# Where operands lie: split weights shifted by 0 to 28 bytes from unit to unit, rows of moving operands a multiple of 256 bytes apart

## The chip, the cores and the metric

The kernel runs on one core of a Trainium2 chip. The metric is the device time of one execution in microseconds (us); less is better. A NeuronCore has a matrix engine (PE, with its weight loads shown as PEld), VectorE (DVE), ScalarE (ACT), GpSimd (POOL) and SyncE (SP). SP and POOL issue nearly all the DMAs here. SBUF is the on-chip memory, 128 partitions wide; an address below is a byte offset within each partition.

## The reference

Two layers of a decoder trunk on 528 tokens (16 learned meta tokens, then 512) with 1024 channels, in float32. Each layer is a half-step SwiGLU feed-forward block, a mixer, and a second half-step SwiGLU block; layer 0 mixes by retention, layer 1 by gated linear attention (GLA):

```python
for i in range(DEPTH):                      # 2
    h = h + 0.5 * swiglu(rmsnorm(h, norm_ffn1[i]), ffn1_w_in[i], ffn1_w_out[i])
    hn = rmsnorm(h, norm_mix[i])
    mix = retention(hn, ...) if i % 2 == 0 else gla(hn, ...)
    h = h + mix
    h = h + 0.5 * swiglu(rmsnorm(h, norm_ffn2[i]), ffn2_w_in[i], ffn2_w_out[i])
h = rmsnorm(h, final_norm)[:, N_META:]

def swiglu(x, w_in, w_out):
    gate, up = jnp.split(x @ w_in, 2, axis=-1)      # 2 x 2816 columns
    return (jax.nn.silu(gate) * up) @ w_out
```

Nearly all the arithmetic is in products of the 528 token columns with weight matrices.

## The kernel before

**Products.** Each fp32 operand is split into a high part in the type fp32r and a low part that is the remainder, also in fp32r. A product of two 128-row blocks is then three matmuls, recorded by the helper `mm3`: high weights by high data (L402), high weights by low data (L403), low weights by high data (L404). Most have 264 moving columns, half of the 528 tokens; in the last feed-forward block they have 256, in GLA 256 or 272. Each matmul has a weight load of 128 columns of its own, so the order on PE is load, matmul, load, matmul, the next load running while a matmul streams.

**Units.** A two-by-two block product (two weight blocks, two halves of the tokens) is done with seven products instead of eight, by the Strassen-Winograd sums. The seven are named `a11, s1, s2, a12, s3, s4, a22`. Their weights are sums of weight blocks, made by GpSimd DMAs that add while they copy and by DVE (L166, L168). Their moving operands are, for three of them, plain rows of the normalized stream (`uha` and `ula`, 8 rows of 528 columns), and for four of them sums over blocks of it, `n3, t1, t2, t4`, kept in `th` (high) and `tl` (low) as `[P, 4, 4, 264]`, the first 4 the row `k` of the product, the second 4 which of the sums. On the way out of a feed-forward block the hidden activations are kept likewise, seven sums of 264 columns in a tile `H` (`hf` in the profile) with the high parts in front and the low parts behind. One product of a unit with four rows `k` is 12 matmuls in the order k = 0 high, low, high; k = 1 high, low, high; and so on.

**Weights.** The class `Weights` streams them. `plan` lists the products' weights in the order of use. `_load` issues a 256 KB DMA on SP into one of `raw_bufs=7` tiles `raw` (and into three `pair` tiles for the sums) as soon as a tile is free. `_split` turns each into a high tile `whi` by an ACT cast (L160) and a low tile `wlo` by a DVE subtraction (L161), four products ahead of PE. There are seven tiles of each, 512 columns of 4 bytes each.

**Addresses.** A row of 264 columns is 1056 bytes, that is 4 x 256 + 32. A row of 528 columns is 2112 bytes, 8 x 256 + 64. The rows `k` of `th` and `tl` are 4224 bytes apart, 16 x 256 + 128, and the low half of `H` lies 7392 bytes behind the high half, 28 x 256 + 224. A weight tile is 2048 bytes and a weight block of 128 columns 512 bytes. In the program as built, all weight blocks of the products start at a multiple of 64 bytes (nearly all of them at a multiple of 256), and all their moving rows at a multiple of 32. What follows calls the difference between the start of a matmul's moving row and the start of the weights that are loaded while it streams, modulo 256 bytes, the relative place of that matmul.

**Order.** The program is recorded in the order of the code with a scheduler that moves urgent instructions ahead; each engine then runs its own instructions in order and waits on semaphores. `causal`, a triangular mask, and `ctail`, three small pieces of it, are loaded and copied once at the start (L355 to L359) and used by retention alone. `half_neg`, eight columns of -0.5, is the exponent for the reciprocal root that POOL computes in the norms.

Of the kernel before, what the change touches and what calls it, by code (L numbers as in the profile page):

```python
# [10 lines left out]
F32 = mybir.dt.float32  # L11
# [3 lines left out]
ALU = mybir.AluOpType  # L15
# [36 lines left out]
BY_P = ((16, 128, 4, 512), (0, 128, 1, 16))  # L52
PW = 512
AHEAD = 4
HEAD_START = 300
# [7 lines left out]
class Weights:  # L63
# [72 lines left out]
    def _split(self, upto):  # L136
        V = self.nc.vector
        while self.split < min(upto, len(self.plan)):
# [80 lines left out]
def trunk(ctx, tc, a):  # L219
# [5 lines left out]
    upool = ctx.enter_context(tc.tile_pool(name="upool", bufs=1))  # L225
    tmp = ctx.enter_context(tc.tile_pool(name="tmp", bufs=2))
    acc = ctx.enter_context(tc.tile_pool(name="acc", bufs=2, space=bass.MemoryType.PSUM))
    W = Weights(tc, ctx)


# [123 lines left out]
    nc.sync.dma_start(ident, a["tri"][0])  # L354
    causal = const.tile([P, P], F32, name="causal")  # L355
    nc.sync.dma_start(causal, a["tri"][1])
    ctail = const.tile([3 * MR, MR], F32, name="ctail")
    for g in range(3):
        S.copy(ctail[g * MR:(g + 1) * MR], causal[g * MR:(g + 1) * MR, g * MR:(g + 1) * MR])  # L359
    ones_r = const.tile([P, P], F32R, name="ones")  # L360
# [13 lines left out]
    uh, ul = [[t[:, d, :] for d in range(KD)] for t in (uha, ula)]  # L374
    rb = upool.tile([P, T], F32, tag="rb", name="rb")
    rc = upool.tile([P, 8], F32, tag="rc", name="rc")

# [60 lines left out]
    def rsqrt_rows(sq, parts, width, name, finish):  # L438
# [10 lines left out]
        ms = tmp.tile([P, 8], F32, tag="ms", name=f"ms_{name}")  # L449
        V.tensor_scalar(ms[:w, :nj], st[:w, :nj], 1.0 / width, EPS, ALU.mult, ALU.add)  # L450
        r = tmp.tile([P, 8], F32, tag="r", name=f"r_{name}")
        G.tensor_tensor(r[:w, :nj], ms[:w, :nj], half_neg[:w, :nj], ALU.pow)
        dg = tmp.tile([P, T], F32, tag="hf", name=f"dg_{name}")
# [11 lines left out]
    def enter(gcol, by, lag=1, lag2=1):  # L465
# [52 lines left out]
        def stats():  # L518
# [12 lines left out]
            for (b0, w, nb, m), c in zip(by, cols):  # L531
                ms = tmp.tile([P, 8], F32, tag="ms", name=f"ms_{name}{c}")
                V.tensor_scalar(ms[:w, :nb], st[:w, c:c + nb], 1.0 / D, EPS, ALU.mult, ALU.add)
                r = rc[:w, c:c + nb]
                G.tensor_tensor(r, ms[:w, :nb], half_neg[:w, :nb], ALU.pow)
# [106 lines left out]
    def quarters(halves, th, tl):  # L642

        tl = tl if isinstance(tl, list) else [tl[:, k] for k in range(4)]
        wd = width(halves)

        def rhs(what, k):
# [3 lines left out]
            i = ("n3", "t1", "t2", "t4").index(what)  # L651
            return th[:, k, i, :wd], tl[k][:, i, :wd]

# [3 lines left out]
    def ffn(which, layer, halves, gcol, feed, late=False):  # L657
# [4 lines left out]
        wd = a1 - a0  # L662
        with tc.tile_pool(name=f"h_{me}", bufs=4) as hp, tc.tile_pool(name=f"t_{me}", bufs=1) as tp, \
# [24 lines left out]
            def sums(j):  # L688
                norm(j)
                for i in range(2):  # L690
                    k = 2 * j + i
                    u_sums(up_, f"{me}{k}", halves, normed[j][:, i].rearrange("p h t -> p (h t)"), th[:, k], tl[:, k])

# [16 lines left out]
            def hidden(f, y, part=None):  # L710
# [265 lines left out]
    def out_last(key, hh, hl, halves, scale):  # L976
# [77 lines left out]
        with tc.issue_after(ins.ins):  # L1054
            for d in range(KD - 4, KD):
                turn(d)
        ms = tmp.tile([P, 8], F32, tag="ms", name="ms_fb")
        V.tensor_scalar(ms[:, :2], st[:, :2], 1.0 / D, EPS, ALU.mult, ALU.add)
        r = tmp.tile([P, 8], F32, tag="r", name="r_fb")
        G.tensor_tensor(r[:, :2], ms[:, :2], half_neg[:, :2], ALU.pow)  # L1060
        for b in range(2):
# [14 lines left out]
    def retention(feed):  # L1076
        with tc.tile_pool(name="retp", bufs=1) as rp, tc.tile_pool(name="wmore", bufs=2) as wp, psum_pool(4) as pp:
# [14 lines left out]
            def sums(k):  # L1092
# [7 lines left out]
                u_sums(rp, f"r{k}", HALVES, un.rearrange("p h t -> p (h t)"), th[:, k], tl[:, k])  # L1100

# [16 lines left out]
            def head(h):  # L1118
# [289 lines left out]
    def gla(feed):  # L1408
        with tc.tile_pool(name="glap", bufs=1) as gp, psum_pool(2) as pp, \
# [4 lines left out]
            for k in range(4):  # L1414
                nc.sync.dma_start(spilt[k], xs[k])
            th = gp.tile([P, 4, 4, 264], F32R, tag="th", name="gth")
            tl, normed = [], []
# [4 lines left out]
            def sums(k):  # L1422
# [15 lines left out]
                tl.append(resid.tile([P, 4, 264], F32R, tag=f"x{k}", name=f"gtl{k}"))  # L1438
                split(th[:, k, :2], tl[k][:, :2], t01)
                split(th[:, k, 2:], tl[k][:, 2:], t23)  # L1440

# [640 lines left out]
```

## Time and profile before

| | |
|---|---|
| median of 3 runs | 2070.59 us (2070.3 to 2073.34) |
| profiled execution, its own time | 2071.41 us |
| its span on the core | 2069.6 us |
| granted TensorE clock | 0.999 of full |
| PE busy | 2057.5 us (99%), 16335 matmuls |
| PEld busy | 2012.9 us (97%), 16335 loads |
| DVE busy | 1790.8 us (87%) |
| ACT busy | 1200.2 us (58%) |
| DMA | 318.84 MB, mean 154 GB/s |

The profile is of one execution. A matmul's recorded duration (about 285 ns) is its passage through the array and overlaps with its neighbours', so the rate at which PE works is not read from durations or from busy time, but from the distance between starts of successive matmuls. The chain of waits is followed back from the last instruction; a chain that is nearly all PE means that a microsecond saved elsewhere is worth nothing unless PE waits for it.

### The profile page before, as it was taken

To read this page: it belongs to the slowest core of one execution; us is meant where nothing else is said; L and a number is where in the kernel's file an instruction comes from. 1 tells how busy PE (TensorE), PEld (TensorE's weight loads), DVE (VectorE), ACT (ScalarE), POOL (GpSimd) and SP (SyncE) were. 2 spreads that over 40 slices of the span, in tenths; PEclk is the share of its full clock that TensorE was granted. 3 is DMA by queue.
4 is the path that set the end of the run, shared out by engine and by line. 5 is a ranking of instruction groups with operands and counts; after the bars stand their busy time and mean duration, and the time that the engine had idled before them with its cause. 6 is when DMAs were issued, how large, how long until landed. Compare 5 with 4: busy or idle time off the path is not lost.

```text
span 2069.6 us, 42946 instructions
## 1 busy us (share of the span) xinstructions
PE 2057.5 (99%) x16335; PEld 2012.9 (97%) x16335; DVE 1790.8 (87%) x3218; ACT 1200.2 (58%) x2365; POOL 208.8 (10%) x181
## 2 busy tenths in 40 slices
PE   9999999999999999999999999999999999999998
PEld 9999999999999999999999999999999988999998
DVE  8988889978686889988889998889897968998886
ACT  5756566554545455656666565666645445666664
POOL 1011111010101000111111011111001000111110
PEclk9999999999999999999999999999999999999999
DMA  7676777355555532776776476677614351687772
GB/s 224 154 193 158 193 185 185 107 144 132 146 132 138 136 104 70 184 191 158 195 188 172 111 180 179 162 197 177 194 57 119 91 165 61 161 214 174 183 179 72
DMA packets 176112, 318.84 MB, mean 154 GB/s; under 512 B 17569, under 2 KB 40737, under 8 KB 175905
## 3 DMA queue, kind: packets, MB, share of 16 engines
q1 hardware_dynamic: 133856, 237.04, 34.6%
q0 software_dynamic: 40896, 75.51, 23.5%
q10 hardware_dynamic: 1152, 3.55, 0.5%
q8 instruction: 128, 2.10, 0.4%
q14 instruction: 80, 0.65, 0.1%
HBM read 311.76 MB, written 4.26 MB: 153 GB/s over the span
## 4 chain that ended last, share of the span: by engine, by line
PE 95%; DVE 2%; ACT 1%; issue 1%; DMA 0%; POOL 0%; SPq 0%; POOLq 0%; ACTq 0%; DVEq 0%
PE po_r L403 2%; PE po_r L402 2%; PE po_r L404 2%; PE Xf20o L402 1%; PE Xf10o L402 1%; PE Xf11o L402 1%; PE Xf10o L404 1%; PE Xf10o L403 1%; PE Xf20o L403 1%; PE Xf20o L404 1%; PE Xf11o L403 1%; PE Xf11o L404 1%; PE lv L1614 1%; PE Xf20u L402 1%; PE Xf11u L402 1%; PE Xf21u L404 1%
## 5 line engine op out<-in xcount | busy, mean ns | idle before, releaser
L160 ACT CAST whi<-raw 128x512 fp32r<-128x512 f32 (+1 forms) x893 | 525.6, 606 | 482.3 <-DVE raw L166 92.2
L161 DVE TENSOR_TENSOR wlo<-raw,whi 128x512 fp32r<-128x512 f32 (+1 forms) x893 | 584.1, 669 | 143.8 <-ACT whi L160 134.7
L160 ACT CAST whi<-pair 128x512 fp32r<-128x512 f32 (+1 forms) x304 | 183.5, 604 | 122.2 <-PE Xf11u L403 7.3
L161 DVE TENSOR_TENSOR wlo<-pair,whi 128x512 fp32r<-128x512 f32 (+1 forms) x304 | 202.0, 664 | 6.4 <-ACT whi L160 5.0
L129 POOL DMA_DIRECT2D pair<-in_f_in x73 | 88.5, 1213 | 725.4 <-DVE wlo L161 313.6
L166 DVE TENSOR_TENSOR raw<-pair,raw 128x512 f32<-128x512 f32 (+1 forms) x146 | 97.3, 667 | 2.6
L168 DVE TENSOR_TENSOR raw<-raw,raw 128x512 f32<-128x512 f32 (+1 forms) x146 | 97.3, 666 | 2.5
L129 POOL DMA_DIRECT2D pair<-in_f_out x44 | 53.2, 1208 | 379.1 <-DVE wlo L161 208.8
L402 PE MATMUL po_r<-ogh,whi 128*128 128x264 f32 x256 | 73.0, 285 | 0.0
L403 PE MATMUL po_r<-ogl,whi 128*128 128x264 f32 x256 | 73.0, 285 | 0.0
L404 PE MATMUL po_r<-ogh,wlo 128*128 128x264 f32 x256 | 72.8, 285 | 0.0
L129 POOL DMA_DIRECT2D pair<-in_ret_in x20 | 24.3, 1215 | 301.8 <-DVE wlo L161 90.7
L402 PE MATMUL Xf20o<-hf,whi 128*128 128x264 f32 x176 | 50.8, 289 | 0.2
L402 PE MATMUL Xf11o<-hf,whi 128*128 128x264 f32 x176 | 50.8, 289 | 0.2
L402 PE MATMUL Xf10o<-hf,whi 128*128 128x264 f32 x176 | 50.8, 289 | 0.2
L403 PE MATMUL Xf10o<-hf,whi 128*128 128x264 f32 x176 | 50.0, 284 | 0.0
L403 PE MATMUL Xf11o<-hf,whi 128*128 128x264 f32 x176 | 50.0, 284 | 0.0
L403 PE MATMUL Xf20o<-hf,whi 128*128 128x264 f32 x176 | 50.0, 284 | 0.0
L404 PE MATMUL Xf10o<-hf,wlo 128*128 128x264 f32 x176 | 49.9, 284 | 0.0
L404 PE MATMUL Xf11o<-hf,wlo 128*128 128x264 f32 x176 | 49.9, 284 | 0.0
L404 PE MATMUL Xf20o<-hf,wlo 128*128 128x264 f32 x176 | 49.9, 284 | 0.0
L402 PEld LDWEIGHTS po_r<-ogh,whi 128*128 128x128 f32 x256 | 48.3, 189 | 0.0
(1007 smaller groups left out, 8523.8 us busy)
## 6 DMA issues: line engine op xcount, KB each, us to landing
raw<-in_f_in SPq DMA_DIRECT2D x277, 256.0 KB, 4.5
pair<-in_f_in SPq DMA_DIRECT2D x150, 256.0 KB, 4.7
pair<-in_f_in POOLq DMA_DIRECT2D x73, 512.0 KB, 6.7
raw<-in_f_out SPq DMA_DIRECT2D x80, 256.0 KB, 3.7
raw<-in_ret_in SPq DMA_DIRECT2D x76, 256.0 KB, 3.3
raw<-in_f_out SPq DMA_DIRECT2D x72, 192.0 KB, 3.2
pair<-in_f_out SPq DMA_DIRECT2D x48, 256.0 KB, 3.9
pair<-in_f_out POOLq DMA_DIRECT2D x24, 512.0 KB, 6.1
```

What stands on the lines that cost most here:

```text
L129: nc.gpsimd.dma_start(t, aps[2].unsqueeze(1).broadcast_to([P, 2, n]), accum_op=ALU.add)
L160: self.nc.scalar.copy(hi[:, :n], raw)
L161: V.tensor_sub(lo[:, :n], raw, hi[:, :n].bitcast(F32))
L166: V.tensor_add(s2, self.tiles[c][:, 1], self.tiles[c, "a11"])
L168: V.tensor_add(raw, raw, s2)
L402: nc.tensor.matmul(ps, lhsT=lh, rhs=rh, start=start, stop=False, **kw)
L403: nc.tensor.matmul(ps, lhsT=lh, rhs=rl, start=False, stop=False, **kw)
L404: return nc.tensor.matmul(ps, lhsT=ll, rhs=rh, start=False, stop=stop, **kw)
L1614: nc.tensor.matmul(ps[:, j, J * P:J * P + n], lhsT=Kt[:, j, J * P:(J + 1) * P], rhs=q, start=(J == 0), stop=(J == 3), skip_group_check=True)
```

## The change

The tiles of the split weights get 8 columns more, 2080 bytes (8 x 256 + 32), and the part that is used starts `c % 8` columns of 4 bytes inside, where `c` counts the units; so all seven products of a unit are shifted by the same 0 to 28 bytes and the next unit by 4 more. Plain (non-unit) weights are not shifted. A tile `wskew` of 32 bytes between the high and the low tiles gives both the same place modulo 256. `th` and `tl` become four tiles each, of 1088 columns (4352 bytes, 17 x 256), so that the rows `k` of one sum lie a multiple of 256 bytes apart; `H` gets 1856 columns a half (7424 bytes, 29 x 256), so that its low part has the place of its high part. The four rows of the head outputs `og` get 16 columns more each. Fillers of 96 and 224 bytes stand behind `th` and `tl`, in the feed-forward blocks and in retention. What this costs in memory is taken from `raw_bufs` (7 to 6), from `causal` and `ctail`, which now live in retention's own pool and are loaded when it is entered, and from `half_neg`, whose exponent is now one column of `rc`. Pools are opened in another order. Number and sizes of matmuls, casts and subtractions are unchanged.

```diff
+SKEW = 4 * 264 + 32
+HW = 7 * 264 + 8
+RSKEW = 56
...
-    def __init__(self, tc, ctx, raw_bufs=7, pair_bufs=3, bufs=7):
+    def __init__(self, tc, ctx, raw_bufs=6, pair_bufs=3, bufs=7):
...
-            hi = home[0].tile([P, PW], F32R, tag="hi", name=f"whi{i}")
-            lo = home[0].tile([P, PW], F32R, tag="lo", name=f"wlo{i}")
+            o = c % 8 if order else 0
+            hi = home[0].tile([P, PW + 8], F32R, tag="hi", name=f"whi{i}")[:, o:o + PW]
+            if i == 0:
+                self.pool.tile([P, 8], F32, tag="skew", name="wskew", bufs=1)
+            lo = home[0].tile([P, PW + 8], F32R, tag="lo", name=f"wlo{i}")[:, o:o + PW]
...
-    half_neg = const.tile([P, 8], F32, name="half_neg")
-    V.memset(half_neg, -0.5)
+    V.memset(rc[:, 7:8], -0.5)
+
+    def rsqrt(r, ms):
+        G.tensor_tensor(r, ms, rc[:r.shape[0], 7:8].broadcast_to(list(r.shape)), ALU.pow)
+
+    def slices(pool, tag, name):
+
+        return [pool.tile([P, SKEW], F32R, tag=f"{tag}{k}", name=f"{name}{k}")[:, :4 * 264]
+                .rearrange("p (i t) -> p i t", i=4) for k in range(4)]
...
-            th, tl = [tp.tile([P, 4, 4, 264], F32R, tag=f"t{i}", name=f"t{i}{me}") for i in "hl"]
+            th, tl = [slices(tp, f"t{i}", f"t{i}{me}") for i in "hl"]
+            tp.tile([P, 24], F32, tag="skew", name=f"skew{me}")
...
-                    h = hp.tile([P, 2, 7, 264], F32R, tag="H", name=f"h{me}{f}")
+                    h = hp.tile([P, 2, HW], F32R, tag="H", name=f"h{me}{f}")[:, :, :7 * 264]
+                    h = h.rearrange("p i (q t) -> p i q t", q=7)
...
-            th, tl = [rp.tile([P, 4, 4, 264], F32R, tag=f"t{i}", name=f"rt{i}") for i in "hl"]
+            th, tl = [slices(rp, f"t{i}", f"rt{i}") for i in "hl"]
+            causal = rp.tile([P, P], F32, tag="causal", name="causal")
+            nc.sync.dma_start(causal, a["tri"][1])
+            ctail = rp.tile([3 * MR, MR], F32, tag="ctail", name="ctail")
+            for g in range(3):
+                S.copy(ctail[g * MR:(g + 1) * MR], causal[g * MR:(g + 1) * MR, g * MR:(g + 1) * MR])
+            rp.tile([P, RSKEW], F32, tag="skew", name="rskew")
...
-                    og[h] = [rp.tile([P, 4, T], F32R, tag="v" + i, name=f"og{i}{h}") for i in "hl"]
+                    og[h] = [rp.tile([P, 4, T + 16], F32R, tag="v" + i, name=f"og{i}{h}")[:, :, :T] for i in "hl"]
```

In the program as built, the three-matmul products keep their order on PE but for two swaps of a few matmuls (in the first feed-forward block and in retention's first head). In both kernels 14,872 of the fp32r matmuls have 256 to 272 columns. By relative place in eighths of 256 bytes (from 0 to 31, 32 to 63 and so on) they number 1719, 2072, 1679, 2033, 1723, 2010, 1625, 2011 before, each eighth then holding one place only, its lower end; and 2136, 1751, 2548, 1569, 2003, 1722, 1765, 1378 in the changed kernel, where any multiple of 4 bytes occurs.

On SP, at the entry to GLA, before (the numbers behind `raw` count the raw loads in order of use; `spill` saves the residual stream):

```order
L132 DMA raw422_19534<-in_f1_out 128x512
L123 DMA pair172_19913<-in_gla_in 128x512 x2
L132 DMA raw423_19575<-in_f1_out 128x512
L132 DMA raw424_19594<-in_gla_in 128x512
L123 DMA pair173_20147<-in_gla_in 128x512 x2
L132 DMA raw425_19670<-in_gla_in 128x512
L132 DMA raw426_19714<-in_gla_in 128x512
L132 DMA raw427_19733<-in_gla_in 128x512
L1415 DMA spill0_19987<-x0_79 128x1056
L1415 DMA spill1_19988<-x1_80 128x1056
```

and in the changed kernel:

```order
L135 DMA raw421_19566<-in_f1_out 128x512
L126 DMA pair172_19945<-in_gla_in 128x512 x2
L135 DMA raw422_19607<-in_f1_out 128x512
L135 DMA raw423_19626<-in_f1_out 128x512
L126 DMA pair173_20182<-in_gla_in 128x512 x2
L135 DMA raw424_19702<-in_gla_in 128x512
L135 DMA raw425_19746<-in_gla_in 128x512
L135 DMA raw426_19765<-in_gla_in 128x512
L1432 DMA spill0_20019<-x0_85 128x1056
L1432 DMA spill1_20020<-x1_86 128x1056
```

Every raw load is issued one place later against the rest of the queue, since it needs a tile that one release more has to free.

On ACT, at the entry to retention, before (`rb` is the row of reciprocal roots that the norm needs):

```order
L489 ACTIVATE sq_n2_7_4941<-x3_82 128x528
L160 CAST whi232_5001<-raw112_4844 128x512
L160 CAST whi233_5007<-raw113_4863 128x512
L160 CAST whi234_5013<-raw114_4881 128x512
L160 CAST whi235_5062<-raw115_4905 128x512
L160 CAST whi236_5108<-raw116_4929 128x512
L546 COPY rb_137<-bc_n2_0_5068 128x512
```

and in the changed kernel:

```order
L499 ACTIVATE sq_n2_7_4946<-x3_88 128x528
L166 CAST whi232_5019<-raw112_4868 128x512
L166 CAST whi233_5025<-raw113_4886 128x512
L1098 COPY ctail_4973<-causal_4971 32x32 x3
L166 CAST whi234_5031<-raw114_4910 128x512
L166 CAST whi235_5080<-raw115_4934 128x512
L556 COPY rb_133<-bc_n2_0_5086 128x512
```

The three small copies of the mask, which stood among the first casts of the program, now stand between two weight casts, and wait for the mask's DMA, which SP issues just ahead of retention's tables `ropeq` and `ropek`; one weight cast that stood ahead of `rb` now stands behind it.

More of the change, by code (lines that the diff above doesn't have):

```diff
@@ L225, in trunk @@
     upool = ctx.enter_context(tc.tile_pool(name="upool", bufs=1))
-    tmp = ctx.enter_context(tc.tile_pool(name="tmp", bufs=2))
+    small = ctx.enter_context(tc.tile_pool(name="small", bufs=2))
     acc = ctx.enter_context(tc.tile_pool(name="acc", bufs=2, space=bass.MemoryType.PSUM))
     W = Weights(tc, ctx)
+    rows = ctx.enter_context(tc.tile_pool(name="rows", bufs=1))
+    tmp = ctx.enter_context(tc.tile_pool(name="tmp", bufs=2))
     def ffn_steps(last, late):
@@ L354, in trunk @@
     nc.sync.dma_start(ident, a["tri"][0])
[L355 to L359, printed above, removed]
     ones_r = const.tile([P, P], F32R, name="ones")
@@ L374, in trunk @@
     uh, ul = [[t[:, d, :] for d in range(KD)] for t in (uha, ula)]
-    rb = upool.tile([P, T], F32, tag="rb", name="rb")
-    rc = upool.tile([P, 8], F32, tag="rc", name="rc")
+    rb = rows.tile([P, T], F32, tag="rb", name="rb")
+    rc = rows.tile([P, 8], F32, tag="rc", name="rc")
+    V.memset(rc[:, 7:8], -0.5)
[4 more added lines that the diff above has]
+                .rearrange("p (i t) -> p i t", i=4) for k in range(4)]
     def urgent():
@@ L448, in rsqrt_rows @@
                              start=(j == 0), stop=(j == nj - 1), skip_group_check=True)
-        ms = tmp.tile([P, 8], F32, tag="ms", name=f"ms_{name}")
+        ms = small.tile([P, 8], F32, tag="ms", name=f"ms_{name}")
         V.tensor_scalar(ms[:w, :nj], st[:w, :nj], 1.0 / width, EPS, ALU.mult, ALU.add)
         r = tmp.tile([P, 8], F32, tag="r", name=f"r_{name}")
-        G.tensor_tensor(r[:w, :nj], ms[:w, :nj], half_neg[:w, :nj], ALU.pow)
+        rsqrt(r[:w, :nj], ms[:w, :nj])
         dg = tmp.tile([P, T], F32, tag="hf", name=f"dg_{name}")
@@ L531, in stats @@
             for (b0, w, nb, m), c in zip(by, cols):
-                ms = tmp.tile([P, 8], F32, tag="ms", name=f"ms_{name}{c}")
+                ms = small.tile([P, 8], F32, tag="ms", name=f"ms_{name}{c}")
                 V.tensor_scalar(ms[:w, :nb], st[:w, c:c + nb], 1.0 / D, EPS, ALU.mult, ALU.add)
                 r = rc[:w, c:c + nb]
-                G.tensor_tensor(r, ms[:w, :nb], half_neg[:w, :nb], ALU.pow)
+                rsqrt(r, ms[:w, :nb])
                 n = m // nb
@@ L642, in quarters @@
     def quarters(halves, th, tl):
-        tl = tl if isinstance(tl, list) else [tl[:, k] for k in range(4)]
         wd = width(halves)
@@ L662, in ffn @@
         wd = a1 - a0
[L663 removed]
+        with tc.tile_pool(name=f"t_{me}", bufs=1) as tp, tc.tile_pool(name=f"h_{me}", bufs=4) as hp, \
                 tc.tile_pool(name=f"u_{me}", bufs=3) as up_, psum_pool(4) as pp:
             other["pool"] = pp
[L666 removed]
+            th, tl = [slices(tp, f"t{i}", f"t{i}{me}") for i in "hl"]
+            tp.tile([P, 24], F32, tag="skew", name=f"skew{me}")
             rhs_in = quarters(halves, th, tl)
@@ L1056, in out_last @@
                 turn(d)
-        ms = tmp.tile([P, 8], F32, tag="ms", name="ms_fb")
+        ms = small.tile([P, 8], F32, tag="ms", name="ms_fb")
         V.tensor_scalar(ms[:, :2], st[:, :2], 1.0 / D, EPS, ALU.mult, ALU.add)
         r = tmp.tile([P, 8], F32, tag="r", name="r_fb")
-        G.tensor_tensor(r[:, :2], ms[:, :2], half_neg[:, :2], ALU.pow)
+        rsqrt(r[:, :2], ms[:, :2])
         for b in range(2):
@@ L1415, in gla @@
                 nc.sync.dma_start(spilt[k], xs[k])
-            th = gp.tile([P, 4, 4, 264], F32R, tag="th", name="gth")
+            th = slices(gp, "th", "gth")
             tl, normed = [], []
```

10 lines of the change are left out of this document (5 added, 5 removed).

## Prediction

> **What bounds the kernel now.** I read the page first, for the shares and the chain, then windows without a stall, for the rate of PE, then the timeline of single products, for what that rate depends on, and last the waits and DMA issues at the two places where the change moves an instruction.
>
> From the page: busy time of PE, its weight loads and DVE, the chain, and the two costliest groups.
>
> ```profile
> PE 2057.5 (99%) x16335; PEld 2012.9 (97%) x16335; DVE 1790.8 (87%) x3218; ACT 1200.2 (58%) x2365; POOL 208.8 (10%) x181
> ...
> PE 95%; DVE 2%; ACT 1%; issue 1%; DMA 0%; POOL 0%; SPq 0%; POOLq 0%; ACTq 0%; DVEq 0%
> ...
> L160 ACT CAST whi<-raw 128x512 fp32r<-128x512 f32 (+1 forms) x893 | 525.6, 606 | 482.3 <-DVE raw L166 92.2
> L161 DVE TENSOR_TENSOR wlo<-raw,whi 128x512 fp32r<-128x512 f32 (+1 forms) x893 | 584.1, 669 | 143.8 <-ACT whi L160 134.7
> ```
>
> The chain is PE for 95% of the span: only the rate of PE and the few places where PE waits count. The rate stands in windows inside layers 0 and 1 in which every matmul has 264 columns (busy time and count of PE, PEld, DVE, ACT, POOL, then the granted clock):
>
> ```profile
> 900.00:980.00 80.00, 80.00 (x659) 80.00 (x659) 69.14 (x118) 47.84 (x92) 9.69 (x8) 1.00 0.69 169
> 1235.00:1315.00 80.00, 80.00 (x660) 80.00 (x659) 67.48 (x113) 46.30 (x89) 9.66 (x8) 1.00 0.70 177
> ```
>
> 80 us over 659 matmuls, of which one or two only reach in at an edge, is 121.5 ns from start to start, at the full clock and without a gap. Times 14,872 matmuls of 256 to 272 columns this is 1807 us, 87% of the span. One ns in that distance is 14.9 us, or 0.7%; the 0.2% that a measurement of this kernel can tell from no change is 4.1 us, or 0.28 ns.
>
> Is the distance a constant? The weight load alone doesn't set it: in a run of ten products with 128 moving columns (from the chain: start, us, count) a load and a matmul take 109 ns together, less than 121.5.
>
> ```profile
> 512.78 1.09 PE tv L1237 x10
> ```
>
> So the moving stream sets it, and where operands lie shows in it. The timeline of PE (start, recorded duration) for the product of `t4` in two units of the same block: the same 12 matmuls on the same rows of `th`, at relative places 96, 224, 96, 224 for k = 0 to 3. First matmul of the product and first one after it; of the second unit the first six too. Last, a product of `t2` (places 64 and 192) and of `t1` (32 and 160).
>
> ```profile
> 1172.19 0.28 PE L402 MATMUL Xf11u<-thf,whi 128*128 128x264 f32 x1
> ...
> 1173.64 0.28 PE L402 MATMUL Xf11g<-uha,whi 128*128 128x264 f32 x1
> ...
> 1192.63 0.29 PE L402 MATMUL Xf11u<-thf,whi 128*128 128x264 f32 x1
> 1192.75 0.29 PE L403 MATMUL Xf11u<-tlf,whi 128*128 128x264 f32 x1
> 1192.88 0.29 PE L404 MATMUL Xf11u<-thf,wlo 128*128 128x264 f32 x1
> 1193.01 0.28 PE L402 MATMUL Xf11u<-thf,whi 128*128 128x264 f32 x1
> 1193.13 0.28 PE L403 MATMUL Xf11u<-tlf,whi 128*128 128x264 f32 x1
> 1193.25 0.28 PE L404 MATMUL Xf11u<-thf,wlo 128*128 128x264 f32 x1
> 1193.37 0.29 PE L402 MATMUL Xf11u<-thf,whi 128*128 128x264 f32 x1
> ...
> 1194.11 0.28 PE L402 MATMUL Xf11g<-uha,whi 128*128 128x264 f32 x1
> ...
> 1176.57 0.28 PE L402 MATMUL Xf11g<-thf,whi 128*128 128x264 f32 x1
> ...
> 1178.03 0.28 PE L402 MATMUL QZf11g<-uha,whi 128*128 128x264 f32 x1
> ...
> 1185.33 0.29 PE L402 MATMUL QZf11u<-thf,whi 128*128 128x264 f32 x1
> ...
> 1186.80 0.28 PE L402 MATMUL Xf11u<-thf,whi 128*128 128x264 f32 x1
> ```
>
> The twelve take 1.45, 1.48, 1.46 and 1.47 us: 120.8, 123.3, 121.7 and 122.5 ns each. Within the slow one the three at place 96 take 0.38 us (127 ns each) and the next three, at 224, 0.36 us (120 ns). So there is something to win or lose here, the place has to do with it, and the same places can run in a fast or in a slow pattern. It is also little: the fastest of these products lies 0.7 ns under the mean, the slowest 1.8 ns over it.
>
> A rule of the Trainium skill speaks to this. "TensorE: Matmul & The Clock Gate", in "Step-by-step: what each phase is for", gives PE two independent SBUF read ports, one for the moving operand and one for weight loads, so that a load doesn't slow the running matmul; by that rule the place of one against the other can't matter, and this change does nothing to the rate. The same page's "Back-to-back issue gap" would put a matmul of 264 columns at 264/2.4 + 2.5 = 112.5 ns. The trace disagrees with both here: 121.5 ns, and 120 against 127 by place.
>
> **The change part by part.**
>
> *The places of the operands.* No matmul, load, cast or subtraction is added or taken away; what can change is the 121.5 ns. In the old program the relative place is always one of the eight multiples of 32 and goes through all of them about evenly (1625 to 2072 matmuls each); the four products above visit six of the eight. In the new one it goes through all multiples of 4, again about evenly (1378 to 2548 in an eighth), because the shift goes round by units and the weight tiles themselves now step by 32 bytes. If the distance depends on the place smoothly, the mean over an even round is the same sum with finer steps: change 0. What the trace can't show is a place that isn't a multiple of 32, since the old program has none. I bound it by the products above: all 14,872 at the rate of the fastest, (120.8 - 121.5) x 14,872 = -10 us; all at the rate of the slowest, (123.3 - 121.5) x 14,872 = +27 us. I take 0: the change picks no place, it spreads them.
>
> *Shifted weights on ACT and DVE.* 1197 casts and as many subtractions now write to addresses that aren't multiples of 32. I take their 606 and 669 ns as unchanged. If they grew by 5%, DVE would gain 40 us of work, spread over 279 us in which it is idle, and PE waits for weights hardly anywhere: cost 0, as long as DVE stays under 100%.
>
> *One raw tile fewer.* SP waits with raw loads for a free tile nearly all the time, up to 23.8 us for one, and a load lands 4.5 us after its issue (SP queue's waits, in all, times, longest; DMA issues):
>
> ```profile
> SPq L132 <- DVE raw L168: 882.3, 140, 23.8
> ...
> raw<-in_f_in SPq DMA_DIRECT2D x277, 256.0 KB, 4.5
> ```
>
> A unit takes 84 x 121.5 ns = 10.2 us and uses three raw tiles, so a tile is worth 3.4 us of lead, and seven are 24 us. A tile is held from its landing through the four products of splitting ahead, some 6 us, and an `a12` until `s4` is made, some 4 us more; with six tiles 20 - 10 - 4.5 leaves about 6 us to spare inside a block. Cost 0 there. At the entry to GLA the cover is thin already. ACT's casts in a row, its wait for a raw load, and the chain there (start, us):
>
> ```profile
> 1466.67 2.71 ACT L160 CAST whi<-raw 128x512 fp32r<-128x512 f32 x5
> ...
> 1472.36 0.62 ACT L160 CAST whi<-raw 128x512 fp32r<-128x512 f32 x1 [2.27 <-DMA raw<-in_gla_in]
> ...
> 1468.01 4.27 DMA raw<-in_gla_in
> ```
>
> ```profile
> 1465.00:1470.00 5.00, 5.00 (x43) 5.00 (x43) 5.00 (x10) 4.30 (x10) 0.00 (x0) 1.00 0.79 246
> 1470.00:1475.00 5.00, 5.00 (x37) 4.69 (x37) 4.01 (x8) 2.73 (x7) 1.20 (x1) 1.00 0.90 293
> 1475.00:1480.00 5.00, 4.06 (x27) 3.49 (x26) 3.25 (x8) 2.54 (x5) 1.71 (x2) 1.00 1.06 360
> ```
>
> This DMA is the one on the chain; behind it PE starts 37 and 27 matmuls in 5 us instead of 43. With six tiles the load waits for one release more. Casts follow each other every 0.54 us there, so +0.5 us is what I take; the ends are 0, if another load is the late one, and 1.5, if the release waits for a whole product.
>
> *The mask at retention's entry.* SP issues one small DMA more ahead of the tables, and the queue behind it (the tables, then six raw loads) moves by an issue of 0.33 us. ACT's three copies wait for its landing; behind them stand two weight casts and `rb`. In the old run, the tables' issue on SP, ACT's cast that would be next, and PE in these windows:
>
> ```profile
> 355.99 0.33 SPq L1090 DMA_DIRECT2D ropeq<-in_rope  x1
> ...
> 358.19 1.64 ACT L160 CAST whi<-raw 128x512 fp32r<-128x512 f32 x3
> 361.89 0.62 ACT L160 CAST whi<-raw 128x512 fp32r<-128x512 f32 x1 [2.06 <-PE pq L403]
> ```
>
> ACT stands 2.06 us here for PE to free a tile, so the copies (0.6 us) and a landing up to 361.9, that is 5.9 us after issue, are hidden: 0. End: +1.5, if the mask lands later. The three copies and the DMA that go from the start of the program were beside PE's start-up work: 0.
>
> Sum against the profiled execution's own 2071.41: 0 + 0.5 = 2071.9. That execution lies 0.8 above the median of the runs, 2070.59, so I forecast 2071 for the median.
>
> **The rivals.**
>
> *A slow place that lasts (slower).* In the old layout a product leaves its place after every third matmul: 96, 224, 96, 224 above. With rows 256 bytes apart and the low parts on the places of the high ones, all 12 matmuls of a product keep one place, so a product that comes to lie near 96 stays at 127 ns, and one near 224 at 120. The rows moved so (`th`, `tl`, `H`) carry some 8600 matmuls. If a quarter of these run at 126 instead of 121.5 ns and a quarter at 120: 2150 x 4.5 - 2150 x 1.5 = +6.5 us, 2077; if slow patterns also catch their neighbours, half of them at 126, +16 us, 2087. For it: the 0.38 us above, and that the slow pattern returns at k = 2 in that same product. Against it: with the same rows the first unit ran in 1.45 us. It decides from a mean of +0.28 ns on.
>
> *Off the 32-byte steps it runs smoother (faster).* All old places are multiples of 32, and a slow pattern may need them: two streams that go through the memory in step. If the shift breaks it, products run like the fastest, 120.8 ns: -10 us, 2061. For it: 1.45 and 1.48 us for one and the same product show that the slow pattern isn't a must. Against it: plain weights aren't shifted, and one unit in eight has shift 0.
>
> *Six raw tiles are too few (slower).* If the entries to the other blocks too lose a release each, five more of up to 1.5 us: 2078. Against it: ACT waits for a raw load in this size at GLA alone.
>
> *The change does nothing to the rate.* Then 2071 as well. The skill's two ports would make it so, against the rows above.
>
> **How the numbers follow.** That the places average out: 0.38, of which 0.29 end within 0.2% (2066.5 to 2074.7), 0.06 above and 0.03 below. A slow place that lasts: 0.31. Smoother off the steps: 0.26. Too few raw tiles: 0.05, 0.01 of it within 0.2%. So faster 0.03 + 0.26 = 0.29, same 0.30, slower 0.06 + 0.31 + 0.04 = 0.41. The likeliest alone ends between 2065 and 2077. For eight in ten the range goes down to 2057, a little past the fastest product's rate, and up to 2087, the slow place with its neighbours.
>
> **What would show it.** Windows as at 900 to 980 with 659 matmuls in 80 us: places averaged out. 655 or fewer: the slow place, and then single products at 1.50 us or more. 663 or more: smoother. `whi` casts at 606 and `wlo` at 669 ns: the shift is free for ACT and DVE. ACT's wait for the raw load at GLA's entry near 2.8 us instead of 2.27. The wrong step would most likely be the first: places between the multiples of 32, which no row here shows.

## The result and the profile after

The changed kernel takes 2085.47 us (median of 4 runs, 2079.66 to 2087.96) against 2070.45 for the kernel before beside it (2069.67 to 2073.34): ratio 1.0068, 95% interval 1.0056 to 1.0080, slower. The profiled execution took 2087.96, with a span of 2086.2 us.

Its page: busy time and counts, the chain, and the two costliest groups.

```profile
PE 2066.2 (99%) x16335; PEld 2019.1 (97%) x16335; DVE 1791.6 (86%) x3218; ACT 1199.9 (58%) x2365; POOL 209.2 (10%) x181
...
PE 89%; DVE 6%; ACT 2%; issue 1%; DMA 1%; POOL 0%; SPq 0%; POOLq 0%; DVEq 0%; ACTq 0%
...
L166 ACT CAST whi<-raw 128x512 fp32r<-128x512 f32 (+1 forms) x893 | 526.5, 606 | 501.1 <-DVE raw L172 92.1
L167 DVE TENSOR_TENSOR wlo<-raw,whi 128x512 fp32r<-128x512 f32 (+1 forms) x893 | 585.8, 671 | 147.3 <-ACT whi L166 140.3
```

The chain has gone from PE 95% and DVE 2% to PE 89% and DVE 6%: PE now stands behind splits and activations. Casts and subtractions have kept their durations. The windows of the prediction (PE, PEld, DVE, ACT, POOL busy, granted clock, DMA):

```profile
900.00:980.00 80.00, 80.00 (x661) 80.00 (x661) 68.43 (x116) 46.20 (x89) 9.69 (x8) 1.00 0.70 174
1235.00:1315.00 80.00, 80.00 (x659) 79.91 (x659) 68.79 (x117) 46.31 (x89) 9.75 (x9) 1.00 0.73 186
```

661 and 659 matmuls, 659 and 660 before: inside the blocks the rate is the same, or a trace better. So the time is lost elsewhere. PE's waits in the whole program (us in all, times, longest):

```profile
PE pf10g L414 <- DVE wlo L167: 2.2, 2, 1.7
PE Xrqkk L412 <- ACT surqkk L630: 1.9, 2, 1.3
PE st_n L534 <- DVE sqa_n L505: 1.7, 1, 1.7
PE pf11g L412 <- ACT uha L488: 1.2, 1, 1.2
...
PE pq L413 <- DVE ula L490: 0.7, 2, 0.4
```

Before, no wait but the one at the program's start was as long as 1 us; the longest after that one was the one at the GLA entry:

```profile
PE st_n L524 <- DVE sqa_n L495: 0.9, 1, 0.9
```

The waits of the changed kernel stand in five places: the start (45 to 49 us), the retention entry (359 to 362), retention itself (468), the entry of the second layer (1134 to 1137) and the GLA entry (1488 to 1491). Laid matmul by matmul beside the trace of before, the lag grows by about 1.5 us in the first, 4.7 and 1.5 at retention, 6.3 and 2.0 at the last two, and by less than 1 us in all between them up to there. At the end it is 16.6 us.

How the retention entry came to be late, from the timelines of ACT (start, us, and in brackets the idle time before), and of SP one issue of a raw load. Before:

```profile
350.56 3.23 ACT L160 CAST whi<-raw 128x512 fp32r<-128x512 f32 x6
354.86 0.62 ACT L160 CAST whi<-raw 128x512 fp32r<-128x512 f32 x1 [1.08 <-DMA raw<-in_ret_in]
355.84 0.74 ACT L478 ACTIVATE uha<-x,gains 128x528 fp32r<-128x528 f32 x1 [0.36 <-DVE x L875]
...
351.25 0.33 SPq L132 DMA_DIRECT2D raw<-in_ret_in  x1
```

After, ACT, then SP's issues of the raw loads, then the matmul that waits:

```profile
351.59 2.70 ACT L166 CAST whi<-raw 128x512 fp32r<-128x512 f32 x5
356.96 0.62 ACT L166 CAST whi<-raw 128x512 fp32r<-128x512 f32 x1 [2.66 <-PE Xf10o L414]
358.33 0.62 ACT L166 CAST whi<-raw 128x512 fp32r<-128x512 f32 x1 [0.76 <-DVE wlo L167]
358.86 0.73 ACT L488 ACTIVATE uha<-x,gains 128x528 fp32r<-128x528 f32 x1
...
352.28 0.33 SPq L135 DMA_DIRECT2D raw<-in_ret_in  x1
...
353.50 3.22 SPq L135 DMA_DIRECT2D raw<-in_ret_in  x5
...
359.64 0.39 PE L412 MATMUL pq<-uha,whi 128*128 128x264 f32 x1 [0.61 <-ACT uha L488]
```

With seven tiles ACT cast six in a row and waited 1.08 us for the seventh. With six it casts five in a row, and then waits twice, 2.66 and 0.76 us. The last cast ahead of `uha` takes the same weights in both kernels. Their load was issued at 351.25 before and landed 3.5 us after that. Now the place in SP's queue at 352.28 goes to the load ahead of it, which the sixth cast waits for and which lands 4.6 us after its issue. The load of those weights is issued only at 353.50, when one more subtraction has freed a tile, and lands 4.7 us after that. With the 1 us of lag that the kernel has by then taken off, it is issued 1.2 us later than before and takes 1.2 us longer. ACT takes its queue in order, so `uha`, which PE needs at the entry, starts at 358.86 instead of 355.84. (The brackets name PE and DVE here; those releases fell within 0.1 us of the landings. In four of the kernels below, e1, e3, e4 and e9, the bracket at the sixth cast names the raw load.)

Then the clock. Windows at three of the places, the wait first and what follows second; the columns end with the granted clock, the DMA share and GB/s:

```profile
359.00:362.10 3.10, 1.76 (x9) 1.26 (x9) 2.48 (x4) 3.10 (x6) 0.46 (x1) 0.98 1.01 372
362.10:369.00 6.90, 6.90 (x35) 6.87 (x34) 4.16 (x10) 2.00 (x6) 1.92 (x2) 0.52 0.90 246
...
1134.00:1136.90 2.90, 1.27 (x9) 0.86 (x7) 0.95 (x2) 2.23 (x4) 0.62 (x1) 0.98 0.98 320
1136.90:1147.20 10.30, 10.30 (x43) 9.62 (x44) 5.04 (x11) 2.46 (x5) 1.92 (x2) 0.51 0.47 119
1488.50:1492.00 3.50, 1.81 (x15) 1.51 (x14) 2.67 (x7) 1.39 (x3) 0.00 (x0) 0.97 1.05 397
1492.00:1495.40 3.40, 3.40 (x13) 2.97 (x12) 2.48 (x7) 1.85 (x3) 1.92 (x2) 0.53 1.10 258
```

Behind these three waits PE runs at half its clock for 6.83, 10.24 and 3.41 us. Matmuls of 264 columns start 220 ns apart there instead of 121.5, so 20.5 us at half clock cost some 8.3 us (and not 9.2, since PE also waits within them). The trace of before has no such stretch ahead of the program's end.

Put together from the starts of all 14,906 matmuls of 256 to 272 columns (34 of them not counted in the prediction) and of the other shapes, against before: distances over 150 ns (waits and half clock) +16.6 us, the other shapes +3.0, which goes with the waits below, and distances up to 150 ns, the pace proper, -3.0. So waits proper make 19.6 - 8.3 = 11.3 us. The columns of the table are worked out in this way for each kernel; the median is of all its runs, the other columns are of its one profiled execution.

| kernel | median, us | lag at the end of the trace | waits and half clock | of this at half clock (us so spent) | pace |
|---|---|---|---|---|---|
| before | 2070.45 | 0 | 0 | 0 (0) | 0 |
| changed | 2085.47 | +16.6 | +19.6 | 8.3 (20.5) | -3.0 |
| e1, before with six raw tiles | 2082.51 | +11.1 | +11.2 | 3.0 (6.8) | -0.1 |
| e2, changed with seven raw tiles | 2070.85 | -1.2 | +0.7 | 0 (0) | -1.9 |
| e3, changed without shift | 2086.14 | +17.0 | +16.8 | 4.5 (10.2) | +0.2 |
| e4, changed, mask early | 2083.46 | +11.2 | +14.5 | 5.7 (13.7) | -3.3 |
| e5, place 128, seven tiles | 2070.15 | -0.4 | +1.1 | 0 (0) | -1.6 |
| e6, place 64, seven tiles | 2068.87 | -3.4 | -0.8 | 0 (0) | -2.6 |
| e7, before with late entries | 2084.15 | +13.1 | +13.2 | at most 7.6 (17.1) | -0.1 |
| e8, changed, shift 4 bytes | 2085.55 (one run) | +14.2 | +16.1 | 5.6 (13.7) | -1.9 |
| e9, changed, shift 16 bytes | 2077.84 (one run) | +6.5 | +12.5 | 1.5 (3.4) | -6.0 |
| e10, seven tiles, all at 16 bytes | 2069.64 | -1.7 | +0.6 | 0 (0) | -2.3 |
| e11, the same, `th` padded | 2070.12 | -0.5 | +0.6 | 0 (0) | -1.1 |

### The profile page after: what moved, and what is told of

It reads as the page before. It is cut to its first block, busy times and chain, and to the rows that moved or that the text cites. A ratio compares the mean times of both kernels' runs of the same rounds, so it can differ in the third digit from the quotient of the medians.

```text
span 2086.2 us, 42933 instructions
## 1 busy us (share of the span) xinstructions
PE 2066.2 (99%) x16335; PEld 2019.1 (97%) x16335; DVE 1791.6 (86%) x3218; ACT 1199.9 (58%) x2365; POOL 209.2 (10%) x181
## 4 chain that ended last, share of the span: by engine, by line
PE 89%; DVE 6%; ACT 2%; issue 1%; DMA 1%; POOL 0%; SPq 0%; POOLq 0%; DVEq 0%; ACTq 0%
DVE wlo L167 2%; PE po_r L413 1%; PE po_r L414 1%; PE po_r L412 1%; PE Xf10o L412 1%; PE Xf10o L413 1%; PE Xf10o L414 1%; PE lv L1631 1%; PE Xf21u L412 1%; PE Xf21u L413 1%; PE Xf21u L414 1%; PE Xf11u L412 1%; PE Xf20u L412 1%; PE Xf21o L412 1%; PE Xf11u L414 1%
## 5 line engine op out<-in xcount | busy, mean ns | idle before, releaser
L413 PEld LDWEIGHTS po_r<-ogl,whi 128*128 128x128 f32 x256 | 48.1, 188 | 0.5 <-DVE ogl L446 0.5
```

The source lines that it names most:

```text
L413: nc.tensor.matmul(ps, lhsT=lh, rhs=rl, start=False, stop=False, **kw)
```

## The experiments

### Is it the raw tile?

e1, the kernel before with one number changed:

```
-    def __init__(self, tc, ctx, raw_bufs=7, pair_bufs=3, bufs=7):
+    def __init__(self, tc, ctx, raw_bufs=6, pair_bufs=3, bufs=7):
```

> The kernel before with six raw tiles in place of seven, and nothing else of the change. Theory R (the sixth raw tile sets the loss): four waits of TensorE appear as in the changed kernel, near 45 us (2.5 us, for the split weights of pf10g), at the retention entry near 359 us (2 to 2.5 us, for uha and ula), at the entry of the next block near 1128 us (2 to 3 us) and longer at the GLA entry near 1477 us, and after each of the last three the granted clock goes to 0.5 for some microseconds; 2084 to 2092 us. Theory L (the new layout of the tiles, and with it which memory a new pool takes over from an old one, makes the waits, and the sixth raw tile is innocent): no such waits, 2069 to 2074 us. In both the pace of 264-column matmuls stays at the kernel before's (820 to 822 in 900 to 1000 us).

Measured: 2082.51 us (2080.97 to 2088.73), ratio 1.0067 [1.0054, 1.0080]; 1.5 us under what theory R gave. PE's waits, ACT at the retention entry, and windows at the last two places:

```profile
PE pf10g L404 <- DVE wlo L161: 2.1, 2, 1.6
PE Xrqkk L402 <- ACT surqkk L620: 1.8, 2, 1.0
PE st_n L524 <- DVE sqa_n L495: 1.7, 1, 1.7
```

```profile
352.47 2.71 ACT L160 CAST whi<-raw 128x512 fp32r<-128x512 f32 x5
357.16 0.62 ACT L160 CAST whi<-raw 128x512 fp32r<-128x512 f32 x1 [1.99 <-DMA raw<-in_ret_in]
```

```profile
1133.90:1137.30 3.40, 2.71 (x19) 2.42 (x19) 2.84 (x5) 1.72 (x4) 0.00 (x0) 0.97 1.06 222
1137.30:1140.80 3.50, 3.50 (x18) 3.50 (x19) 1.88 (x6) 0.62 (x1) 1.92 (x2) 0.54 0.66 188
1484.50:1488.90 4.40, 2.71 (x20) 2.57 (x20) 3.01 (x7) 1.67 (x5) 1.07 (x1) 0.97 1.07 327
1488.90:1492.40 3.50, 3.50 (x14) 3.02 (x13) 2.13 (x5) 1.15 (x3) 0.85 (x2) 0.55 0.99 304
```

The same places, the same five casts in a row, the bracket naming the raw load, and the clock halved at two of the three places that were foretold (at the retention entry it stayed at 1.00). None of the new layout is in this kernel. Theory R holds, theory L is out.

e2, the changed kernel with seven tiles; for the room the padding of the slices goes:

```
-SKEW = 4 * 264 + 32
+SKEW = 4 * 264
...
-    def __init__(self, tc, ctx, raw_bufs=6, pair_bufs=3, bufs=7):
+    def __init__(self, tc, ctx, raw_bufs=7, pair_bufs=3, bufs=7):
```

> The changed kernel with seven raw tiles again; for the room the slices of the moving operands lose their padding (rows 4224 bytes apart, not 4352), the weights' shift of 0 to 28 bytes stays. Theory R: the four waits and the halved clock are gone, and what is left is the gain in pace of the shifted weights, 0.2 to 0.35 ns on each of 14,872 matmuls: 2065 to 2069 us. Theory L: the waits stay, 2081 to 2089 us. If the pace came from rows at multiples of 256 bytes and not from the shift, 2069 to 2073 us and 820 to 822 matmuls in 900 to 1000 us.

Measured: 2070.85 us, ratio 1.0003 [0.9994, 1.0012]. ACT at the retention entry:

```profile
350.10 3.23 ACT L166 CAST whi<-raw 128x512 fp32r<-128x512 f32 x6
354.26 0.62 ACT L166 CAST whi<-raw 128x512 fp32r<-128x512 f32 x1 [0.94 <-DMA raw<-in_ret_in]
355.38 0.74 ACT L488 ACTIVATE uha<-x,gains 128x528 fp32r<-128x528 f32 x1 [0.50 <-DVE x L886]
```

Six casts in a row again, no stretch at half clock, and the loss is gone. The gain that I expected on top isn't there: the pace is 1.9 us better in the trace, half of what I took, and the median of 11 runs shows none of it. This edit takes the padding away too, but e5 below keeps slices 4352 bytes apart with seven tiles and shows no loss either, so it isn't the padding that cost.

e4, the changed kernel with the mask loaded and copied at the start, as before:

```
+    causal = const.tile([P, P], F32, name="causal")
+    nc.sync.dma_start(causal, a["tri"][1])
...
-            causal = rp.tile([P, P], F32, tag="causal", name="causal")
-            nc.sync.dma_start(causal, a["tri"][1])
```

> The changed kernel with the causal mask loaded and its tail copied at the start again, as before; six raw tiles, shift and padding as changed. Theory R and theory L alike: one transfer and three copies of ScalarE less at the retention entry, 0 to 1.5 us off the changed kernel beside it, the wait of TensorE for uha and ula near 359 us still there. If the mask in the queue of SyncE is what makes the retention entry late: 4 to 6 us off, the wait gone, and the granted clock there 1.00.

Measured: 2083.46 us, ratio to before 1.0065 [1.0052, 1.0078], which overlaps that of the changed kernel. The waits at the retention entry stand, and ACT's late `surqkk` too:

```profile
PE Xrqkk L417 <- ACT surqkk L635: 1.3, 2, 0.8
...
PE pq L418 <- DVE ula L495: 0.7, 2, 0.4
```

So the mask is not what makes the entry late. Whether it costs nothing or 2 us can't be told: the executions of one and the same kernel with six tiles lie up to some 8 us apart, and the granted clock goes along: the changed kernel's four took 2087.96, 2087.31, 2083.62 and 2079.66 us at mean granted clocks of 0.994, 0.995, 0.997 and 0.998.

### Is it the wait or the clock?

e7 makes PE late with seven raw tiles: the activation that writes `uha` of the seventh piece is repeated at three entries.

```
                 if "h" in parts:
-                    S.activation(hi, src, AF.Copy, scale=g)
+                    more = {G_MIX: 4, G_F1 + 8: 4, G_MIX + 8: 2}.get(gcol, 0) if d == KD - 2 else 0
+                    for _ in range(1 + more):
+                        S.activation(hi, src, AF.Copy, scale=g)
```

> The kernel before with the activation that writes uha of the seventh piece repeated at three entries (four more times at the retention entry and at the entry of the second layer, twice more at the GLA entry; each 0.72 us, the same value written again), so that TensorE waits there although there are seven raw tiles. Theory W (the time lost is the wait alone): 1 to 2.2 us at each of the three, the granted clock 1.00 throughout, 2073.5 to 2077 us. Theory C (a wait of TensorE halves its clock for one stretch of 3.41 us or more, which costs 1.7 us each time besides the wait): one to three stretches at clock 0.5 right behind these places, 2076 to 2083 us.

Measured: 2084.15 us (2083.10 to 2084.59), ratio 1.0065 [1.0053, 1.0078]; 1 us over the most that theory C gave. ACT's repeats at the retention entry, three in one row:

```profile
356.22 1.98 ACT L480 ACTIVATE uha<-x,gains 128x528 fp32r<-128x528 f32 x3
```

Windows, each time the gap first and the stretch behind it second, and last the GLA entry:

```profile
361.00:363.00 2.00, 0.22 (x2) 0.00 (x1) 1.07 (x3) 0.53 (x2) 1.87 (x2) 0.86 1.08 267
362.50:369.50 7.00, 6.20 (x23) 5.16 (x24) 2.65 (x5) 1.15 (x2) 0.55 (x2) 0.52 0.76 222
414.00:417.00 3.00, 0.76 (x7) 0.42 (x4) 2.88 (x7) 2.43 (x5) 0.00 (x0) 1.00 0.75 132
417.00:424.00 7.00, 6.88 (x32) 6.78 (x33) 5.20 (x17) 3.17 (x12) 0.00 (x0) 0.51 0.01 2
1140.00:1144.20 4.20, 2.02 (x11) 1.33 (x11) 2.28 (x6) 0.14 (x2) 1.92 (x2) 0.99 0.75 188
1144.20:1147.70 3.50, 3.50 (x19) 3.50 (x18) 0.00 (x0) 0.65 (x2) 0.00 (x0) 0.53 0.02 6
1475.00:1480.00 5.00, 5.00 (x44) 5.00 (x42) 5.00 (x10) 3.63 (x8) 0.00 (x0) 1.00 0.94 292
```

Three gaps of about 2 us (the second stands 53 us behind the first, where nothing is repeated) are followed by 17.1 us at half clock, with no raw tile taken away. Theory C holds: a short gap of PE costs itself and, often, some microseconds at half clock (here at most 7.6 of the 13.1 us, by 220 ns against 121.5 for all of the 17.1 us, within which PE also waited). At the GLA entry I was wrong: the two repeats found room there and cost nothing.

### What do the places do?

e3, the changed kernel with no shift:

```
-            o = c % 8 if order else 0
+            o = 0
```

> The changed kernel with every weight tile's shift set to 0; rows at multiples of 256 bytes, six raw tiles. If the shift off the 32-byte steps makes the pace (0.2 to 0.35 ns of each of 14,872 matmuls): the pace of the kernel before, 3 to 5 us longer than the changed kernel beside it, 2083 to 2092 us with the same waits. If the padding of the moving rows makes it: the changed kernel's own pace and time, 2080 to 2088 us. If one relative place for all units is slow (the rival of the prediction): 10 us or more longer, 2093 us or above.

e8 and e9, one shift for all units, `o = 1 if order else 0` and `o = 4 if order else 0`:

> The changed kernel with one shift for all units, 4 bytes, in place of 0 to 28 bytes going round. Read by the mean distance of 264-column matmuls from start to start (gaps under 150 ns): 121.43 ns in the changed kernel, 121.76 without a shift. Theory O (any place off the 32-byte steps is smoother): 121.2 to 121.5. Theory T (the going round averages good and bad places, a constant shift does nothing by itself): 121.6 to 121.9. The waits of the changed kernel stay in both: 2078 to 2090 us.

> The same with 16 bytes for all units, the middle between two 32-byte steps. Theory O: 121.2 to 121.5 ns, the same as with 4 bytes or lower. Theory T: 121.6 to 121.9 ns. The waits of the changed kernel stay: 2078 to 2090 us.

Matmuls in 100 to 300 us, a stretch without waits in all of these kernels. Before:

```profile
100.00:300.00 200.00, 200.00 (x1640) 199.70 (x1639) 175.73 (x304) 121.28 (x238) 25.29 (x21) 1.00 0.72 183
```

The changed kernel:

```profile
100.00:300.00 200.00, 200.00 (x1643) 199.67 (x1642) 175.98 (x305) 121.86 (x239) 24.77 (x21) 1.00 0.73 184
```

e3, without a shift:

```profile
100.00:300.00 200.00, 200.00 (x1636) 199.66 (x1635) 175.36 (x303) 120.77 (x237) 24.20 (x20) 1.00 0.72 183
```

e8, 4 bytes:

```profile
100.00:300.00 200.00, 200.00 (x1644) 199.73 (x1643) 176.20 (x306) 121.94 (x239) 25.43 (x21) 1.00 0.73 184
```

e9, 16 bytes:

```profile
100.00:300.00 200.00, 200.00 (x1646) 199.59 (x1646) 176.13 (x306) 121.86 (x239) 25.43 (x21) 1.00 0.72 184
```

Means over all 264-column matmuls with distances under 150 ns: 121.74 ns before, 121.43 changed, 121.76 without the shift, 121.47 with 4 bytes, 121.19 with 16. The same layout, or one in which most tiles lie the same 2048 or 640 bytes elsewhere (e1, e4), gives the same mean in another execution (121.74, 121.75 and 121.74 in before, e1 and e7; 121.43 and 121.41 in the changed kernel and e4), so tenths are real here. In this layout the shift makes the difference and the padded rows alone don't. e3's time can't show it: its median is 0.7 us longer, not the 3.2 that its pace loses, but its profiled execution has half as much time at half clock, and executions of the changed kernel lie 8 us apart. By e8 and e9 theory O looked right: a constant shift does as much or more.

e10 puts this to use with seven raw tiles: e2 with `o = 4` for all weights, plain ones too. e11 pads `th` besides.

> Seven raw tiles, every weight tile (units and plain ones) shifted by 16 bytes, slices of the moving operands 4224 bytes apart (unpadded). Theory O (16 bytes, midway between two 32-byte steps, is the smooth place, whatever the layout): 121.0 to 121.4 ns from start to start, 0.35 to 0.75 ns under the kernel before on 14,872 matmuls, no wait over 1 us at the entries: 2059 to 2066 us. Theory P (the pace belongs to the whole layout, and the one with the 16-byte shift and padded slices happened to be good): 121.5 to 121.8 ns, 2068 to 2072 us.

> The same with the slices th of the FFN and retention padded to 4352 bytes (the pair H and the slices tl are left unpadded for the room). Theory O: 121.0 to 121.4 ns as without the padding, within 2 us of it, 2058 to 2066 us. Theory P: a layout of its own, anywhere from 121.2 to 121.8 ns, more than 0.2 ns apart from the unpadded one, 2063 to 2072 us.

Measured: 2069.64 us, ratio 0.9997 [0.9988, 1.0006], and 2070.12, 0.9995 [0.9986, 1.0004]. The same window in e10:

```profile
100.00:300.00 200.00, 200.00 (x1643) 199.66 (x1642) 175.83 (x303) 121.18 (x239) 25.43 (x21) 1.00 0.72 183
```

Means: 121.53 ns in e10 and 121.65 in e11, not 121.2. The 16 bytes don't carry over to another layout. Theory O falls; the pace belongs to the layout as a whole.

e5 and e6 try the place itself: weights unshifted, seven tiles, slices of `th` and `tl` 4352 bytes apart; the two kernels differ only in that three uses of one tile stand ahead of the weights instead of behind them, which moves these places by 64 bytes.

```
-        sq = tmp.tile([P, T], F32, tag="sqa", name=f"sqa_{name}", bufs=1)
+        sq = small.tile([P, T], F32, tag="sqa", name=f"sqa_{name}", bufs=1)
```

> Seven raw tiles, weights unshifted and 2048 bytes apart as before, the slices of the moving operands th and tl 4352 bytes (17 times 256) apart, and rb and rc moved so that the first row of every slice lies 128 bytes past the weights, modulo 256. The four rows of a slice are 1056 bytes apart, so its products run at 128, 160, 192 and 224, and all matmuls of one product at one place. Theory S (a place has a pace of its own, as read from the kernel before: th at 96 takes 125.6 ns, at 224 119.4): 121.0 ns over the 3947 matmuls on th and tl against 121.9 before, 3 us off, 2066 to 2069 us. Theory N (the place of th and tl changes nothing): 2069.5 to 2072 us. In both no wait over 1 us at the entries.

> The same with one more tile (sqa) moved, so that the first rows lie 64 bytes past the weights: products on th and tl at 64, 96, 128 and 160. Theory S: 122.7 ns over the 3947 matmuls, 3 us more than the kernel before and 6 to 7 us more than with 128 bytes: 2072.5 to 2076 us, matmuls on th in the second row at 125 ns or more. Theory N: as with 128 bytes, within 1 us.

Measured: 2070.15 us, 1.0000 [0.9991, 1.0009], and 2068.87, 0.9995 [0.9986, 1.0004]. The kernel that was to be the slow one is, if anything, the faster. The window from 100 to 300 us has 1642 matmuls in e5 and 1644 in e6.

On `th`, places 128, 160, 192 and 224 took 120.6, 121.8, 123.2 and 120.4 ns in e5; 64, 96, 128 and 160 took 121.1, 121.9, 120.8 and 121.8 in e6. Place 192 was among the fastest before (120.2) and place 96 the slowest by far (124.7). So theory S falls as I put it: a place modulo 256 has no pace of its own. Over all 264-column matmuls it accounts for 5% of the variance of the distance before and 1 to 7% in the other layouts looked at. What else in the layout sets it stays open.

No kernel tried here beats the kernel before by more than a measurement can tell.

## Why the prediction was right or wrong

**The rate of PE.** I took 0, with ends of -10 and +27 us. Measured: -3.0 us, inside the ends and near the value; 661 and 659 matmuls in the windows, as for "averaged out". The mechanism was only half right. The mean over places does stay within a few tenths, but not because each place keeps its pace and an even round sums to the same (e5, e6).

**The shifted weights on ACT and DVE.** Right: 606 and 671 ns, 606 and 669 before. (Not all of the 1197 casts write off the 32-byte steps: in the program as built some 930 do, since plain weights and one unit in eight aren't shifted.)

**One raw tile fewer.** This is the step that failed. I put it at 0 inside the blocks and +0.5 at the GLA entry; e1 shows that it alone costs 12 us (2082.51 against 2070.47), and with seven tiles again the whole loss goes (e2). ACT's own wait at the GLA entry I had nearly right. In the changed kernel:

```profile
1482.39 0.62 ACT L166 CAST whi<-raw 128x512 fp32r<-128x512 f32 x1 [0.30 <-DMA raw<-in_gla_in]
1484.51 0.62 ACT L166 CAST whi<-raw 128x512 fp32r<-128x512 f32 x1 [1.31 <-DMA raw<-in_gla_in]
1486.43 0.62 ACT L166 CAST whi<-raw 128x512 fp32r<-128x512 f32 x1 [1.10 <-DMA raw<-in_gla_in]
```

2.71 us in three parts; I had said near 2.8. PE's wait behind it grew by 0.75 us, from 0.94 to 1.69, near the 0.5 that I took. Three things were missing. First, I reckoned the lead in the steady state (six tiles, some 6 us to spare) and looked for a thin cover at one entry, where a wait for a raw load stood on the chain. At the retention entry the same wait of 1.08 us stood in ACT's timeline of before, hidden by about 1.4 us (`uha` ready at 356.58, taken by PE at 357.97). Second, a tile fewer doesn't cost one cast of 0.54 us there: the load is issued one release, 1.2 us, later and takes 1.2 us longer to land, and ACT's wait grew from 1.08 to 3.42 us in two parts. Third, the half clock, 1.5 to 8.3 us in the kernels with six tiles, of which nothing in the profile of before spoke.

**The mask at retention's entry.** 0, end +1.5. e4 leaves it between 0 and 2 us; the waits don't come from it.

**The rivals.** "A slow place that lasts", to which I gave .31, ends in the same stretch of time and is nevertheless wrong: products of 12 matmuls on `th` and `tl` take 1.456 us in the mean against 1.463 before, and 3 of 289 reach 1.50. In e3, where no unit is shifted against another and a slow place would have cost 10 us more, the mean distance is 121.76 ns, as before (121.74). "Off the 32-byte steps it runs smoother" has its direction from e3, e8 and e9, a third of its size in the changed kernel, and no rule that carries over. "Six raw tiles are too few" was the mechanism, with five entries losing up to 1.5 us each and 2078 us; it had .05. The argument against it, that ACT waits for a raw load "in this size at GLA alone", was no argument: what counts is the slack behind the wait, and that was 1.4 us for `uha` at retention's entry. That the change does nothing to the rate is nearly so, but the layout does set it: means go from 121.19 to 121.76 ns by layout, the same from execution to execution. By the two independent ports of the Trainium skill's "TensorE: Matmul & The Clock Gate" ("Step-by-step: what each phase is for") no place of a moving row against the weights would matter. The trace doesn't tell whether it is these two reads that meet or others, so the rule is neither borne out nor refuted here.

The forecast of 2071 was thus 14 us low. Of that, e1 puts 12 us down to the third term of the sum alone, and e2, which brings all but 0.4 us back, leaves nothing for the others that these runs could tell. That 2085.47 still lies inside the range of 2057 to 2087 is luck: its upper end came from the slow place with its neighbours, which isn't what happened.

## What to carry to other kernels

When a ring of buffers gets a place fewer, don't reckon its lead in the steady state: go to each entry of a block, count the transfers that the in-order engine takes in one run there, and compare the wait for the last of them with the slack of what is queued behind it. A gap of 1 or 2 us on TensorE is to be priced at more than itself, since its clock may halve for some microseconds behind it. And where operand placement moves the pace by tenths of a nanosecond, the memory that the placement takes from a ring can easily cost more than it brings.

## What the runs showed of the hardware that was not expected

The half clock. It came in stretches of 3.41, 6.83 and 10.24 us, and in one execution all of them begin on one grid: in the changed kernel at 361.97, 1136.79 and 1491.78 us, 227.0 and 104.0 times 3.413 us apart. The Trainium skill's "TensorE: Matmul & The Clock Gate" ("Part 1: The HAM clock gate") states a free-running window of 3413 ns, and the trace agrees. The Trainium skill's abstract rule on the same page ("HAM oscillation — how this bites in real kernels") is no idle gaps over about 3.4 us. It is far too lenient here: gaps of 1.7 to 2.1 us at the GLA entry (five kernels), and of 0.42 and 0.32 us within 2 us at the second layer's entry (e1), were followed by half clock. Nor does the gap alone decide: one of 1.65 us that ends near 49 us was followed by none in any of the six kernels with six raw tiles, nor was one of 1.4 us at the GLA entry in e8, nor such a pair of 0.41 and 0.31 us at the retention entry in e1. What does decide stays open; in the fixed grid lies a likely reason why executions of one kernel with six tiles lie up to some 8 us apart, and those of the kernel before within 4.4, but no run here isolates it.

The second is that the pace of 264-column matmuls goes with the memory layout, came back to within 0.02 ns in the mean wherever the layout did (before, e1 and e7; the changed kernel and e4), and yet doesn't follow from the operands' places modulo 256 or 32 bytes (e5, e6, e10).
